# A decoder layer on one core: the down projection as seven block products with weight sums made in DRAM

## The chip, the core and the metric

The kernel runs on one core of a Trainium2 chip. The metric is the device time of one execution in microseconds (us); lower is better. Engine names are those of the profile: PE is the matrix engine, PEld its weight loads, DVE the vector engine, ACT the scalar engine, POOL the general-purpose engine, SP the engine whose queue issues most transfers.

## The reference

One decoder layer on 512 tokens of width 1024 in float32: attention with two branches of 8 heads each (a forgetting softmax branch, "fox", and a stick-breaking branch, "sb"), gates, an output projection, a layer norm, then a gated MLP with a causal convolution of width 3, and a second layer norm. The part that changes is the end:

```python
h_gate, h_val = jnp.split(h, 2, axis=-1)
ffn_out = (jax.nn.silu(h_gate) * h_val) @ w_down
x = _layer_norm(DEEPNORM_ALPHA * x + (1.0 + gt2) * ffn_out, ln2_g, ln2_b)
```

`w_down` is 2816 x 1024, so the product has 512 rows (tokens), an inner dimension of 2816 = 22 x 128 and 1024 columns.

## The kernel before, in words

Every large product is done in three matmuls: each float32 operand is split into a rounded high part (`hi_of`, L74, on ACT) and the rest (`lo_of`, L77, on DVE), and high x high, high x low and low x high are summed in PSUM.

**Weights.** `weights` (L128) is one stream of items of 512 KB for the whole kernel. SP loads them in order into 4 buffers `raw` (L132), ACT makes `wh` (L152) and DVE `wl` (L78 by way of L153) in 3 buffers each. A `raw` buffer is free again when its item has been split; a `wh` buffer when PE has used it. Items are loaded up to 3 ahead of use and split up to 2 ahead.

**Order.** The program is built by a framework that schedules each engine's instructions ahead of time by a model of their costs; SP alone keeps the order of the source. On the chip each engine works through its own list in order, and an instruction that waits holds up all that stand behind it on that engine.

**Stages.** (1) modulation and the first projections; (2) sixteen heads, eight sb then eight fox, in the loop over `heads` (L774), filled up with the remaining projections; each fox head needs two small transfers by POOL (`decay_rows`, L342 and L343); (3) merging of the branches: `merge` (L704) adds on POOL (L706), then splits into `mh` and `ml`; the output weights are scaled on POOL by the gate (`wo_proc`, L601) and split into `woh`, `wol`; (4) output projection and layer norm; (5) the up projection, 44 items of 24 matmuls, each followed by the convolution, and for each pair of items `silu(gate) * value`, split into `hh` and `hl` (L957 to L960); POOL applies the layer norm's row parameters to the residual `x1` in `o_x1` (L887); (6) the down projection: 22 items of `w_down`, each scaled on POOL by the gate (`wdn_proc`, L613), split, and multiplied into 8 PSUM banks (4 blocks of 128 tokens x 2 halves of 512 columns; `down`, L973 to L977). The first 16 items go through all 8 banks; the last 6 (`LATE`) are held split and taken block by block, so that each block's layer norm (L1004 to L1015) runs beside the matmuls of the next. The last half block is cut into two pieces of 256 columns.

SBUF holds 60 buffers `z` of 128 x 512 float32 that all stages share.

Of the kernel before, what the change touches and what calls it, by code (L numbers as in the profile page):

```python
# [16 lines left out]
P = 128  # L17
# [5 lines left out]
FT = DFF // P  # L23
NH = 8
# [13 lines left out]
LATE = 6  # L38
EARLY = 2
# [6 lines left out]
def layer_kernel(ctx: ExitStack, tc: tile.TileContext, out, xT, x, cT, crow, wa0, wa1, bcol, bgt, w1, wct, wv, bf,  # L46
                 wp, wo, lncol, lnrow, wup, cwb, wdn):
# [4 lines left out]
    cons = ctx.enter_context(tc.tile_pool(name="cons", bufs=1))  # L52
    stg = ctx.enter_context(tc.tile_pool(name="stg", bufs=1))
# [74 lines left out]
    def weights(i, ahead=AHEAD):  # L128
        while state["load"] < min(len(items), i + LOADS):
            it = items[state["load"]]  # L130
            it[3] = stg.tile([P, 1024], F32, name=nm("raw"), tag="raw", bufs=LOADS)
            nc.sync.dma_start(it[3][:, 0 : it[2]], it[0])  # L132
            state["load"] += 1
            while state["proc"] <= state["load"] - LOADS:
                process()
# [475 lines left out]
    def wdn_proc(late):  # L611
        def f(r):
            G.tensor_tensor(r, r, gt[1], ALU.mult)  # L613
            if not late:
                h, l = split_proc(r)
                return [h[:, 0:512], h[:, 512:1024]], [l[:, 0:512], l[:, 512:1024]]
            h = [z(F32R, "wdh") for _ in range(2)]
            l = [z(F32R, "wdl") for _ in range(2)]
            for e in range(2):
                c = slice(e * 512, (e + 1) * 512)  # L620
                hi_of(h[e], r[:, c])
                lo_of(l[e], r[:, c], h[e])
            return h, l
# [147 lines left out]
    fill(48)  # L771
    heads = [(br, 2 * p + e) for br, p in seq for e in range(2)]
    last = hd[heads[1]]['last']
    for n, (b, h) in enumerate(heads):  # L774
# [9 lines left out]
        fill(f1)  # L784
        if n + 1 < 16:
# [5 lines left out]
        stage_c(b, h)  # L791
        if n == 7:
# [35 lines left out]
    def ln_row(n):  # L828
# [3 lines left out]
        if n % 2 == 0:  # L832
            for e in range(2):
                G.tensor_scalar(t[e], t[e], -0.5, None, ALU.mult)
# [52 lines left out]
    def o_x1(i):  # L887
        if not lnr:
            lnr.extend([ln_row(0), ln_row(1)])
        for e in range(2):  # L890
            G.tensor_tensor(x1[i][e], x1[i][e], lnr[0][e], ALU.mult)
            G.tensor_tensor(x1[i][e], x1[i][e], lnr[1][e], ALU.add)


    hh, hl = [], []
# [7 lines left out]
    wdi = [add_item(wdn[j], wdn_proc(j >= FT - LATE)) for j in range(FT)]  # L903
# [24 lines left out]

    hc = []
    for n in range(2 * FT):  # L930
# [4 lines left out]
        else:  # L935
# [3 lines left out]
            if n % 2 == 0 and 6 <= n < 14:  # L939
                o_x1((n - 6) // 2)  # L940
            if n in (20, 36):
                g = 6 if n == 20 else 7
                list(ada_split(g, wai[4 * g + 3]))
            if n in (22, 38):
# [5 lines left out]
        hc.append(t)  # L950
        if n % 2 == 1:
# [4 lines left out]
            a, b = z(F32R, "hh"), z(F32R, "hl")  # L956
            hi_of(a, g)  # L957
            lo_of(b, g, a)
            hh.append(a)
            hl.append(b)  # L960
# [4 lines left out]
    lnr = []  # L965
    for i in range(2):
        t = fin.tile([P, D], F32, name=f"ln2_{i}", tag=f"ln2_{i}")
        nc.sync.dma_start(t, lnrow[2 + i : 3 + i, :].broadcast_to([P, D]))
        lnr.append(t)
    G.tensor_scalar(lnr[0], lnr[0], -0.5, None, ALU.mult)  # L970
    acc = [[bank() for _ in range(2)] for _ in range(NB)]

    def down(ps, j, i, w, first, last):  # L973
        tb = slice(i * P, (i + 1) * P)
        PE.matmul(ps, hh[j][:, tb], w[0], start=first, stop=False)  # L975
        PE.matmul(ps, hh[j][:, tb], w[1], start=False, stop=False)  # L976
        PE.matmul(ps, hl[j][:, tb], w[0], start=False, stop=last)  # L977

    own = (NB - 1, 1)
    for j in range(FT - LATE):  # L980
        w = weights(wdi[j])
        for i in range(NB):
            for e in range(2):
                down(acc[i][e], j, i, (w[0][e], w[1][e]), j == 0, (i, e) == own and j == FT - LATE - 1)
    ws = [weights(wdi[j]) for j in range(FT - LATE, FT)]
    for i in range(NB):
        tb = slice(i * P, (i + 1) * P)
        r = x1[i]
# [96 lines left out]
```

## Time and profile before

| what | us |
|---|---|
| median of 3 runs | 765.2 (765.07 to 765.88) |
| span of the profiled execution, first to last instruction | 761.9 |
| what the median has around that span | 3.3 |
| down projection, first to last matmul | 633.9 to 754.1 |
| after the last matmul | 7.8 |

The profiled execution has no time of its own on record beside its span; the median of the runs stands for it. The rows below give busy times per engine, idle time by what ended it, and the time from issue to landing of transfers. A row "a us, b" is total and mean in ns; "x n" is a count; "idle before <-" names what was waited for.

### The profile page before, as it was taken

The page shows a single profiled execution, that of the slowest core. Times are in us where ns is not written, and L with a number is a line of the kernel's source. Part 1 is how long each engine was busy: PE and PEld are TensorE (multiplying, and loading weights), DVE is VectorE, ACT ScalarE, POOL GpSimd, SP SyncE. Part 2 cuts the span into 40 slices and gives each one's busy share as a digit, 9 for nine tenths or more (in the row PEclk, how much of TensorE's full clock was granted, in tenths as well). Part 3 has the DMA queues.
Part 4 walks back from the last instruction along what each step waited for, and adds up shares of the span by engine and source line. Part 5 has one row for each costly group of instructions (what it writes and reads, how often), then busy time and mean ns, then how long its engine had stood idle before and what let it go on. Part 6 is the DMA issues. An engine that isn't in the chain of part 4 may idle for free.

```text
span 761.9 us, 9520 instructions
## 1 busy us (share of the span) xinstructions
PE 747.8 (98%) x3538; PEld 621.3 (82%) x3538; DVE 547.6 (72%) x812; ACT 350.7 (46%) x583; POOL 188.3 (25%) x162
## 2 busy tenths in 40 slices
PE   8999999998999999999999999999999999999995
PEld 4878888877888888888899888888888888888885
DVE  6869799887788985675667697777665765434566
ACT  4567566784866654524145334443444433122300
POOL 1035223542010021362000860000000034845500
PEclk9999999999999999999999999999999999999998
DMA  8944445243332333445203434353323214323202
GB/s 331 405 164 143 162 178 210 83 139 117 106 112 75 120 111 111 138 144 187 90 1 121 156 112 137 111 193 111 139 84 110 84 55 166 139 83 98 97 29 82
DMA packets 31105, 99.68 MB, mean 131 GB/s; under 512 B 4273, under 2 KB 4785, under 8 KB 31058
## 3 DMA queue, kind: packets, MB, share of 16 engines
q1 hardware_dynamic: 30258, 98.72, 36.8%
q8 instruction: 28, 0.46, 0.2%
q10 hardware_dynamic: 288, 0.28, 0.1%
q0 software_dynamic: 512, 0.07, 0.1%
q14 instruction: 19, 0.16, 0.1%
HBM read 96.88 MB, written 2.10 MB: 130 GB/s over the span
## 4 chain that ended last, share of the span: by engine, by line
PE 92%; DVE 4%; DMA 2%; issue 1%; ACT 1%; DVEq 0%; ACTq 0%
PE ps L116 18%; PE ps L118 18%; PE ps L117 18%; PE ps L976 5%; PE ps L975 5%; PE ps L977 5%; PE ps L270 5%; PE ps L521 2%; PE ps L503 2%; PE ps L854 2%; PE ps L855 2%; PE ps L856 2%; DMA raw<-in_wa 1%; PE ps L444 1%; PE ps L445 1%; PE ps L420 1%
## 5 line engine op out<-in xcount | busy, mean ns | idle before, releaser
L78 DVE TENSOR_TENSOR wl<-raw,wh 128x1024 fp32r<-128x1024 f32 (+2 forms) x110 | 150.7, 1371 | 94.5 <-ACT wh L152 94.1
L152 ACT ACTIVATE wh<-raw 128x1024 fp32r<-128x1024 f32 x101 | 106.6, 1057 | 96.8 <-PE ps L977 38.5
L116 PE MATMUL ps<-u2h,wh 128*128 128x512 f32 (+1 forms) x376 | 141.6, 376 | 0.0
L117 PE MATMUL ps<-u2l,wh 128*128 128x512 f32 (+1 forms) x376 | 141.4, 376 | 0.0
L118 PE MATMUL ps<-u2h,wl 128*128 128x512 f32 (+1 forms) x376 | 141.4, 376 | 0.0
L613 POOL TENSOR_TENSOR raw<-raw,gt 128x1024 f32<-128x1024 f32 x22 | 60.1, 2744 | 190.6 <-DVE gt L576 157.7
L117 PEld LDWEIGHTS ps<-u2l,wh 128*128 128x128 f32 x376 | 70.9, 188 | 12.8
L118 PEld LDWEIGHTS ps<-u2h,wl 128*128 128x128 f32 x376 | 70.9, 188 | 12.8
L116 PEld LDWEIGHTS ps<-u2h,wh 128*128 128x128 f32 x376 | 70.9, 188 | 12.6
L116 PE MATMUL ps<-uh,wh 128*128 128x512 f32 x200 | 79.6, 398 | 0.0
L117 PE MATMUL ps<-ul,wh 128*128 128x512 f32 x200 | 78.3, 391 | 0.0
L118 PE MATMUL ps<-uh,wl 128*128 128x512 f32 x200 | 78.2, 391 | 0.0
L976 PE MATMUL ps<-wl,hh 128*128 128x512 f32 x128 | 49.9, 390 | 0.0
L977 PE MATMUL ps<-wh,hl 128*128 128x512 f32 x128 | 49.9, 390 | 0.0
L975 PE MATMUL ps<-wh,hh 128*128 128x512 f32 x128 | 49.9, 390 | 0.0
L483 POOL TENSOR_TENSOR pt<-pt,om 128x127 f32<-128x127 f32 (+3 forms) x32 | 42.7, 1346 | 10.8 <-DVE om L482 9.7
L118 PEld LDWEIGHTS ps<-uh,wl 128*128 128x128 f32 x200 | 37.6, 188 | 8.2
L116 PEld LDWEIGHTS ps<-uh,wh 128*128 128x128 f32 x200 | 37.7, 188 | 7.3
L117 PEld LDWEIGHTS ps<-ul,wh 128*128 128x128 f32 x200 | 37.7, 189 | 7.1
L75 ACT ACTIVATE hh<-cv 128x512 fp32r<-128x512 f32 x22 | 13.9, 631 | 59.6 <-DVE cv L955 59.6
L954 ACT ACTIVATE cv<-cv 128x512 f32<-128x512 f32 x22 | 13.9, 632 | 56.5 <-DVE cv L949 56.5
L601 POOL TENSOR_TENSOR raw<-raw,gt 128x1024 f32<-128x1024 f32 x8 | 20.7, 2596 | 77.1 <-DMA raw<-in_wo 75.9
(185 smaller groups left out, 1511.6 us busy)
## 6 DMA issues: line engine op xcount, KB each, us to landing
raw<-in_wup SPq DMA_DIRECT2D x44, 512.0 KB, 3.2
raw<-in_wa SPq DMA_DIRECT2D x32, 512.0 KB, 3.3
raw<-in_wct SPq DMA_DIRECT2D x25, 512.0 KB, 3.2
raw<-in_wdn SPq DMA_DIRECT2D x22, 512.0 KB, 3.3
wa<-in_wa SPq DMA_DIRECT2D x14, 512.0 KB, 7.9
raw<-in_wv SPq DMA_DIRECT2D x8, 512.0 KB, 3.4
raw<-in_wp SPq DMA_DIRECT2D x8, 512.0 KB, 3.3
raw<-in_wo SPq DMA_DIRECT2D x8, 512.0 KB, 3.2
```

Of the source, the lines that this page charges most:

```text
L78: return V.tensor_tensor(o, i, fl(hi), ALU.subtract)
L116: PE.matmul(ps, wh, ah, start=first, stop=False)
L117: PE.matmul(ps, wh, al, start=False, stop=False)
L118: PE.matmul(ps, wl, ah, start=False, stop=last)
L152: state["hi"] = S.activation(h[:, 0:cols], r[:, 0:cols], AF.Copy)
L270: PE.matmul(grp[g], w, u, start=j == 0 and n == 0, stop=j == KT - 1 and n == (1 if g == 7 else 2))
L483: G.tensor_tensor(pt[b][:, s : e - 1], pt[b][:, s : e - 1], om[:, s + 1 : e], ALU.mult)
L601: G.tensor_tensor(r, r, gt[0], ALU.mult)
L613: G.tensor_tensor(r, r, gt[1], ALU.mult)
L975: PE.matmul(ps, hh[j][:, tb], w[0], start=first, stop=False)
L976: PE.matmul(ps, hh[j][:, tb], w[1], start=False, stop=False)
L977: PE.matmul(ps, hl[j][:, tb], w[0], start=False, stop=last)
```

## The change

The down projection is cut into 2 x 2 x 2 blocks: 2 halves of the tokens (256), the inner blocks taken in 11 pairs (even, odd), 2 halves of the columns (512). A scheme of Strassen's kind then needs 7 block products instead of 8. The sums of activations that it needs are made per pair on POOL in `blocks`, four subtractions or additions of 128 x 256, and then split; the sums of weights are made in DRAM: ACT copies weights to scratch tensors (`down_copy`, one pair per head, in the loop over the heads) and POOL issues transfers that add to what stands there (`down_sum`, written in the up projection's loop). Each of the three transfers of a pair reads what the one before it wrote, and waits for it.

Three operands of each of the first 8 pairs (`oh`, `ol`, `sp`) are stored to DRAM (`keep`) and fetched back into `z` buffers by POOL's queue (`back`); the residual `x1` also goes to DRAM and back. The gate is no longer applied to the weights, but for 6 late items, scaled on POOL and stored in the up stage (`scale_proc`); otherwise it is applied to the results, by POOL in `fold` and by DVE in `gated`. The products come in four parts: A (`ai`, 11 items of 12 matmuls), B (`bi`, 11 of 12), D (`dci`, 5 of 12 and 1 of 6), C (`ci`, 5 of 12), then the last 6 pairs of C row block by row block from `cli`.

In the built program the framework has put all 33 adding transfers of `down_sum` into POOL's list between the fox heads and the first `merge`, not into the up projection.

```diff
+    def down_copy(n, e):
+        if 0 <= n - 5 < FP:
+            with tc.issue_after(state["hi"].ins):
+                S.dma_start((w31, w24)[e][n - 5], wdp[n - 5][:, e * 1024 : (e + 1) * 1024])
+    def down_sum(n):
+        if n < FP:
+            G.dma_start(w31[n], wdp[n][:, 2048:3072], accum_op=ALU.add)
+        if 0 <= n - 1 < FP:
+            G.dma_start(wt2[n - 1], w31[n - 1][:, 0:512], accum_op=ALU.add)
+        if 0 <= n - 2 < FP:
+            G.dma_start(wt4[n - 2], wt2[n - 2], accum_op=ALU.add)
...
-            hi_of(a, g)
-            lo_of(b, g, a)
+            if n % 4 == 3:
+                work = blocks(*hs)
+    def blocks(e, o):
...
+        hi_of(oh, o)
+        lo_of(ol, o, oh)
+        G.tensor_tensor(g[:, lo], e[:, hi], e[:, lo], ALU.subtract)
+        G.tensor_tensor(g[:, hi], o[:, lo], e[:, lo], ALU.subtract)
+        G.tensor_tensor(e[:, lo], g[:, hi], e[:, hi], ALU.add)
+        G.tensor_tensor(s4[:, lo], o[:, hi], e[:, lo], ALU.subtract)
...
+        hi_of(gh, g)
+        lo_of(gl, g, gh)
...
+        hi_of(eh, e)
+        lo_of(el, e, eh)
+        hi_of(sp[:, lo], s4[:, lo])
+        lo_of(sp[:, hi], s4[:, lo], sp[:, lo])
...
+    def fold(i, e, t, sign):
+        G.tensor_tensor(t, t, (g0, g1)[e], ALU.mult)
+        G.tensor_tensor(r[i][e], r[i][e], t, sign)
...
+    for i in range(2):
+        V.tensor_tensor(u3[i], u2[i], Z[i], ALU.add)
+    for i in range(2):
+        V.tensor_tensor(c22[i], u3[i], W[i], ALU.add)
+        V.tensor_tensor(u2[i], u2[i], W[i], ALU.add)
...
+    for i in range(2):
+        fold(i, 0, u3[i], ALU.add)
+        fold(i, 1, c22[i], ALU.subtract)
...
+    def gated(i, e, ps):
+        t = fine("t")
+        V.tensor_tensor(t, ps, (g0, g1)[e], ALU.mult)
+        V.tensor_tensor(r[i][e], r[i][e], t, ALU.add)
...
+    for p in range(FP - LATE):
+        oh, ol, sp = keeps[p]
+        w = weights(ci[p])
...
+        if p % 2 == 0 and p < 4:
+            fold(2 + p // 2, 1, u2[p // 2], ALU.subtract)
+            first_rows(p // 2)
+    for q in range(LATE):
+        wc[q] = weights(cli[q])
+    for i in range(2):
+        gated(2 + i, 0, X[i])
+        gated(2 + i, 1, W[i])
```

More of the change, by code (lines that the diff above doesn't have):

```diff
@@ L23 @@
 FT = DFF // P
+FP = FT // 2
+H = T // 2
 NH = 8
@@ L38 @@
 LATE = 6
+STAY = 3
 EARLY = 2
@@ L950, in layer_kernel @@
         hc.append(t)
+        if n > 3:
+            next(work, None)
         if n % 2 == 1:
```

252 lines of the change are left out of this document (183 added, 69 removed).

## The prediction

> **What bounds the kernel now.** First the page: its span, the busy time per engine, and the chain of work that ended last, by engine.
>
> ```profile
> span 761.9 us, 9520 instructions
> PE 747.8 (98%) x3538; PEld 621.3 (82%) x3538; DVE 547.6 (72%) x812; ACT 350.7 (46%) x583; POOL 188.3 (25%) x162
> ...
> PE 92%; DVE 4%; DMA 2%; issue 1%; ACT 1%; DVEq 0%; ACTq 0%
> ```
>
> PE carries 92% of the chain. An average over stages can hide another limit in one of them, so next the table by stage for the stretches that the change touches: the heads with the branches' merge, two of the up projection, the down projection, the end.
>
> ```profile
> core 0: us, PE busy (x) PEld busy (x) DVE busy (x) ACT busy (x) POOL busy (x), PEclk, DMA share, GB/s
> 172.00:310.00 138.00, 135.60 (x701) 113.38 (x700) 108.12 (x201) 84.60 (x172) 17.27 (x18) 1.00 0.33 108
> ...
> 405.00:450.00 45.00, 45.00 (x220) 38.12 (x219) 38.10 (x38) 20.29 (x27) 28.93 (x18) 1.00 0.40 141
> 450.00:500.00 50.00, 50.00 (x222) 41.45 (x221) 36.71 (x46) 22.46 (x30) 0.00 (x0) 1.00 0.37 127
> ...
> 633.90:754.10 120.20, 120.16 (x547) 99.97 (x545) 63.92 (x75) 25.10 (x33) 54.86 (x20) 1.00 0.30 106
> ...
> 754.00:762.00 8.00, 0.06 (x1) 0.00 (x0) 4.49 (x13) 0.29 (x1) 0.00 (x0) 0.66 0.19 66
> ```
>
> In the down projection PE is busy for 120.16 of 120.20 us at full granted clock (1.00), while DVE works 63.92 us, half of it. So a matmul less is time less there, but only until DVE has become the busier one. That is the question of this change.
>
> **Step 1, the matmuls: 15.0 us less on PE.** Durations of single matmuls overlap, so their spacing counts. Two rows of PE's timeline, the first and the last of 97 matmuls in a row, and the counts of one of the three product lines:
>
> ```profile
> 609.65 0.39 PE L117 MATMUL ps<-u2l,wh 128*128 128x512 f32 x1
> ...
> 631.41 0.39 PE L117 MATMUL ps<-u2l,wh 128*128 128x512 f32 x1
> ```
> ```profile
> L975 PE MATMUL ps<-wh,hh x128: 388/390/390, 633.9 to 720.3; 128*128 128x512 f32 x128
> ...
> L975 PE MATMUL ps<-wdh,hh x54: 278/389/390, 721.0 to 753.5; 128*128 128x512 f32 x42, 128*128 128x256 f32 x12
> ```
>
> (631.41 - 609.65) / 96 = 0.2267 us. Before: 3 x (128 + 42) = 510 full matmuls and 3 x 12 = 36 half ones; the halves come out at (120.2 - 115.6) / 36 = 0.13 us. After: 7 products x 11 pairs x 2 blocks x 3 = 462, of which 18 are again cut into 36 halves: 444 x 0.2267 + 4.6 = 105.3 us. 66 matmuls go, 66 x 0.2267 = 15.0 us. If PE stays the bound, this is the gain. In times from the stage's start: A ends at 29.9, B at 59.9, D (66 matmuls) at 74.8, C (60) at 88.4, the last rows at 105.3.
>
> **Step 2, DVE from the end of B: it becomes the bound, and takes back 12.1 us.** Rows of DVE and POOL in the stages before, whose operations are those of the new stage:
>
> ```profile
> 457.47 0.69 DVE L955 TENSOR_TENSOR cv<-cv,cv 128x512 f32<-128x512 f32 x1
> ...
> 702.68 1.21 DVE L78 TENSOR_TENSOR wl<-raw,wh 128x1024 fp32r<-128x1024 f32 x1
> 703.82 1.28 DVE L78 TENSOR_TENSOR wdl<-raw,wdh 128x512 fp32r<-128x512 f32 x2
> ...
> 725.31 0.69 DVE L1004 SCALAR_TENSOR_TENSOR xn<-xn,ps 128x512 f32<-128x512 f32 x1 [2.39 <-PE ps L977]
> 726.03 0.69 DVE L1005 BATCH_NORM_STATS2 st<-xn 128x6 f32<-128x512 f32 x1
> ...
> 730.84 0.21 DVE L819 BATCH_NORM_AGGREGATE mv<-st 128x2 f32<-128x12 f32 x1
> ...
> 734.45 0.68 DVE L1004 SCALAR_TENSOR_TENSOR xn<-xn,ps 128x512 f32<-128x512 f32 x1
> ```
> ```profile
> 441.44 1.77 DVE L955 TENSOR_TENSOR cv<-cv,cv 128x512 f32<-128x512 f32 x1
> 443.13 2.32 DVE L78 TENSOR_TENSOR wl<-raw,wh 128x1024 fp32r<-128x1024 f32 x1
> ```
> ```profile
> 302.75 1.30 POOL L706 TENSOR_TENSOR sg<-sg,sg 128x512 f32<-128x512 f32 x1
> ...
> 439.13 3.53 POOL L891 TENSOR_TENSOR xn<-xn,lnr 128x512 f32<-128x512 f32 x2
> 442.62 3.98 POOL L892 TENSOR_TENSOR xn<-xn,lnr 128x512 f32<-128x512 f32 x2
> ```
>
> By the distance to the next start, a full split costs 703.82 - 702.68 = 1.14 us, a half one 0.64, an operation with a PSUM operand or a row statistic 0.72, and a row's norm from its aggregate to its last write 734.45 - 730.84 = 3.6. In the built order DVE, once B's last product is there, has: u3, the split of D's second item and u3 again, which end at 59.9 + 1.3 = 61.2; then four operations on PSUM (2.9); eight full splits and one half (9.1 + 0.6); twelve half splits of the late items (7.7); six `gated` pairs (6 x (0.72 + 0.64) = 8.2); statistics and norms of two rows (4 x 0.72 + 7.2 = 10.1); and, before the last addition, row 2 and the start of row 3: nine operations of 512 columns at 0.72 (6.5) and about 2.3 of small ones (8.8). Sum 47.4, which puts the last addition at 108.6 us with DVE never idle, against 105.3 for PE.
>
> POOL runs beside it: twelve `fold` operations (1.30 us alone), four of them while DVE reads PSUM, eight beside its splits. The four rows at 439 to 443 us show what that does when both read SBUF: 1.77 for 0.69 and 2.32 for 1.23, 1.1 us more each. Eight such delays are 8.7 us (bounds: 0, and 8 x 1.30 = 10.4). The last addition then starts at 61.2 + 47.4 + 8.7 = 117.3 us, where before it started right after PE's last matmul at 120.2. Behind it stands the same end, 7.8 us. **So 2.9 of the 15.0 us are left.** PE will wait in C above all, for the splits of C's items, which stand in DVE's list behind the late items' splits and the two row norms.
>
> **Step 3, the adding transfers on POOL's queue: taken at 0, but with no cover.** The trace of before has no such transfer. Nearest rows, from the list of transfers:
>
> ```profile
> raw<-in_wdn SPq DMA_DIRECT2D x22, 512.0 KB, 3.3
> wa<-in_wa SPq DMA_DIRECT2D x14, 512.0 KB, 7.9
> ...
> xn<-in_x SPq DMA_DIRECT2D x8, 256.0 KB, 2.8
> ...
> s<-chi POOLq DMA_DIRECT2D x8, 4.0 KB, 1.6
> ```
>
> Each pair has one of 512 KB (A us) and two of 256 KB (B us); the second waits on POOL for the first, the third for the second. In the built list they stand ahead of the last fox heads' small transfers, of the output weights' scaling (L601) and of the first merge (L706). Nearest in time are these:
>
> ```profile
> 258.55 0.59 ACT L527 ACTIVATE ytmp<-ps 64x512 f32<-64x512 f32 x1
> ...
> 270.73 0.59 ACT L527 ACTIVATE ytmp<-ps 64x512 f32<-64x512 f32 x1 [2.47 <-PE ps L521]
> ...
> 304.08 0.63 ACT L75 ACTIVATE mh<-sg 128x512 fp32r<-128x512 f32 x1 [4.52 <-POOL sg L706]
> ...
> 307.36 1.06 ACT L152 ACTIVATE wh<-raw 128x1024 fp32r<-128x1024 f32 x1 [0.17 <-PE ps L117]
> ...
> 323.68 1.06 ACT L152 ACTIVATE wh<-raw 128x1024 fp32r<-128x1024 f32 x1 [0.61 <-PE ps L117]
> ```
>
> A head takes 270.73 - 258.55 = 12.2 us, and one pair is copied per head, so POOL keeps up while A + B, with 1 us of issuing, stays under 12.2. The copies of pairs 8 to 10 are issued near 269 to 291. Pair 8 can be added from some 274 on; with the second scaling (2.6), the first merge then ends at about 282 + 3A + 2B. Before it ended at 304.05, and ACT's `mh` waited for it. How late may it be? The two `wh` rows bracket three items on PE (307.2 to 323.1, 5.3 each); the second of these is needed at 312.5, and after the merge ACT and DVE need 3.9 us for it (`mh`, two `woh`, `wh`, `wl`). So a stall is 3A + 2B - 26.6, if positive. Bounds: A from 3.3 (a plain load) to 15.8 (twice the crowded load of 7.9); B from 2.8 to 7.9. I take A = 6.0 and B = 4.3: two loads' time less one latency of 1.6 for the 512 KB (5.0) and for the 256 KB (4.0), and 1 and 0.3 for traffic beside it. That is 26.6, a stall of 0, at the very edge. The heads' small transfers have slack: POOL issued a head's rows at 181, and its scores came at 237.6, 56 us later.
>
> ```profile
> 181.32 0.52 POOL L342 DMA_DIRECT2D s<-chi  x1 [5.20 <-PE ps L450]
> ```
> ```profile
> 237.62 0.24 PE ps L445
> ```
>
> On what an addition costs there is a rule in the Trainium skill, Collectives: The Full Stack, section "The bandwidth ceiling: the fold count and why AG ≠ RS ≠ AR": a reducing transfer has to read two sources, and so runs at half a copy's rate. By it alone A would be 5.0 and B 4.0 and the stall none, the sum the same; no trace of before shows such a transfer.
>
> **Step 4, the rest, taken at 0.** Up projection: per four items (21.8 us) DVE has 36.71 / 50 x 21.8 = 16.0 us, to which come one half split and one of 256 columns (1.05), and up to 2.6 of waiting for four POOL operations (half of 1.30 each): 19.7 of 21.8. At 405 to 450 us DVE was 85% busy beside a busy POOL and PE lost nothing, so that cover holds, narrowly. Parts A and B: an item per 2.72 us needs 1.14 on DVE and 1.06 on ACT, and a load of 3.3 with four buffers. What is fetched back (9 MB in 60 us) doubles the traffic to some 350 GB/s; were one load as late as the 7.9 us row, that is 4.6 us, once. So 0 to 5.
>
> **Sum.** 761.9 of span - 15.0 + 12.1 = 759.0; with the 3.3 us around the span, which I take from the median, **762.3 us** against 765.2, 0.4% faster.
>
> **The rivals.**
> - *Slower: the adding transfers hold POOL.* Above 3A + 2B = 26.6 (A + B about 10.3) the first merge is late, and ACT and then PE behind it; above A + B = 13 the earlier pairs lag too. At A = 9 and B = 6 the last pairs cost 39 - 26.6 = 12.4. The first copy lands near 172 us by its place in ACT's list; eight pairs of 14 us (A + B less the 1 us by which the next pair starts ahead) end at 284, 10 later than the 274 above. Together 22: 762.3 + 22 = 784. At A = 10, B = 7 the same sum gives 43, 805. For: the DMA share is already 0.33 there, 22 copies of 512 KB come on top, and each addition passes through memory more often than a load. Against: at the price of loads, 11 x (3.3 + 2 x 2.8) = 98 us of transfers fit into the 130.
> - *Faster: PE stays the bound.* If DVE and POOL get past each other and DVE's list has less in it than I count, the full 15.0 comes: 750 to 757. Against it: 47.4 us of DVE work in 45.4 of PE's even without a single delay.
> - *No change: DVE is fully shut out.* If each of the eight splits waits for a whole POOL operation, 10.4 goes instead of 8.7: 764.0; with a stall or two of Step 4 up to 767. The Trainium skill, SBUF — State Buffer, section "Who interferes with whom", makes this the rule: the pair of ports that the two engines share is locked for a whole instruction. The rows at 439 to 443 us, with 1.1 for 1.30, come near it.
>
> **How the numbers follow.** About 0.2% (1.5 us) is what a measurement of this kernel can tell from no change. Chances: forecast (758 to 763.6) 0.35; POOL held 0.41; PE the bound 0.11; no change 0.13. So faster 0.35 + 0.11 = 0.46, same 0.13, slower 0.41. At the far bounds (A 15.8, B 7.9) the first rival's sum is over 100 us; I leave 0.15 of it above 788, and 0.05 of the second below 752. Range: 752 to 788. The forecast's own range is 758 to 763.6.
>
> **What would show it.** Step 1: 444 + 36 matmuls in the last stage at the same spacing. Step 2: PE idle in C, ended by `wl`; `wl` at 2.3 us beside `fold`. Step 3: A and B as the time from issue to landing; POOL idle for transfers between 230 and 310 us, and `mh` waiting for POOL. Step 4: no PE idle in the up projection, A and B. Wrong it would be if A + B is over 11, or if C shows no wait of PE.

## The result, and the profile after

The changed kernel takes 791.3 us (median of 4 runs, 788.1 to 795.1) against 765.45 for the kernel before in the same series: a ratio of 1.0344, 95% interval 1.0312 to 1.0376. It is 3.4% slower. The forecast was 762.3 us, 0.4% faster, with a range up to 788; the rival "the adding transfers hold POOL" was priced at 784. The profiled execution is the run of 788.1 us, with a span of 786.4. Line numbers below are those of the changed kernel; a kernel with a few lines more or less shows the same statements one to six lines further up or down.

First the page of the changed kernel: span, busy time per engine, and the engines' shares of the chain that ended last.

```profile
span 786.4 us, 9844 instructions
PE 746.1 (95%) x3472; PEld 614.0 (78%) x3472; DVE 588.9 (75%) x866; ACT 375.4 (48%) x624; POOL 271.3 (35%) x285
...
PE 67%; DVE 12%; DMA 10%; issue 5%; POOL 2%; ACT 2%; SPq 0%; DVEq 0%; POOLq 0%; ACTq 0%
```

PE has 66 instructions fewer and is the chain for 67% of the span, where it was 92%. Transfers now carry 10%. So the time is not in the new products but in waits elsewhere. The table by stretches shows where; first two of the kernel before, cut at the same events, then the changed kernel.

```profile
222.50:296.00 73.50, 73.50 (x394) 62.09 (x393) 58.73 (x113) 43.87 (x93) 6.54 (x4) 1.00 0.29 99
296.00:345.20 49.20, 49.16 (x217) 40.32 (x217) 33.28 (x36) 20.41 (x32) 22.47 (x11) 1.00 0.40 135
```
```profile
core 0: us, PE busy (x) PEld busy (x) DVE busy (x) ACT busy (x) POOL busy (x), PEclk, DMA share, GB/s
...
229.00:304.50 75.50, 74.87 (x393) 61.86 (x393) 61.13 (x116) 43.05 (x92) 15.98 (x18) 1.00 0.92 257
304.50:371.00 66.50, 55.43 (x218) 43.93 (x217) 35.33 (x35) 18.32 (x30) 30.15 (x19) 0.87 0.58 152
...
664.60:694.60 30.00, 30.00 (x134) 24.85 (x133) 20.84 (x21) 15.58 (x19) 20.22 (x30) 1.00 1.03 358
694.60:725.40 30.80, 30.10 (x133) 24.61 (x132) 18.75 (x14) 11.68 (x11) 10.13 (x14) 1.00 0.97 334
725.40:761.00 35.60, 31.34 (x130) 25.10 (x129) 34.42 (x45) 16.90 (x23) 22.35 (x14) 0.95 0.56 183
```

The same 217 or 218 matmuls of the merge stretch take 66.5 us instead of 49.2. In the heads before it the DMA share has gone from 0.29 to 0.92. The down projection's parts A and B run with one wait of PE, 0.70 us in B; in part C (from 725.4) DVE is busy for 34.42 of 35.60 us.

What holds the merge is on POOL. The adding transfers stand in its list from 176.75 us on, among the small transfers of the fox heads. Its timeline, columns start, length, and in brackets the idle time before and what ended it; L797, L799 and L801 are the three adding transfers of a pair, L614 the scaling of the output weights, L724 the merge:

```profile
275.51 0.81 POOL L797 DMA_DIRECT2D w<-in_wdp  x1 [0.84 <-DMA w<-in_wdp]
...
290.16 1.15 POOL L797 DMA_DIRECT2D w<-in_wdp  x1
300.13 0.81 POOL L799 DMA_DIRECT2D w<-w  x1 [8.82 <-DMA w<-in_wdp]
307.08 0.81 POOL L801 DMA_DIRECT2D w<-w  x1 [6.14 <-DMA w<-w]
307.62 2.64 POOL L614 TENSOR_TENSOR raw<-raw,gt 128x1024 f32<-128x1024 f32 x1
...
329.21 0.81 POOL L801 DMA_DIRECT2D w<-w  x1 [3.19 <-DMA w<-w]
329.76 1.55 POOL L724 TENSOR_TENSOR sg<-sg,sg 128x512 f32<-128x512 f32 x1
```

The second scaling starts at 307.62 (282.4 before) and the first merge at 329.76 (302.75 before), each directly behind an adding transfer that waited for the one ahead of it. The list of the tile that the transfers write gives POOL's idle time before all 33 of them, by what ended it (us, times):

```profile
  DMA w<-in_wdp: 66.5, 15
  DMA w<-w: 46.4, 11
```

That is 113 us of waiting between 176 and 329 us. The first kind covers two things, a pair's own first addition and the copies that ACT issues: seven of the fifteen waits, 25 us, ended when a copy landed. The last of these seven is the row at 275.51 above. Behind the merge wait ACT and then PE, in the timelines of these two:

```profile
331.34 0.63 ACT L84 ACTIVATE mh<-sg 128x512 fp32r<-128x512 f32 x1 [23.04 <-POOL sg L724]
```
```profile
334.00 0.79 PE L125 MATMUL ps<-yh,wh 128*128 128x512 f32 x1 [6.15 <-ACT wh L165]
...
337.15 0.63 PE L125 MATMUL ps<-yh,wh 128*128 128x512 f32 x1
337.58 0.63 PE L126 MATMUL ps<-yl,wh 128*128 128x512 f32 x1
```

`wh`, which PE needs, stands behind `mh` in ACT's list. After the wait PE's matmuls come at a spacing of 337.58 - 337.15 = 0.43 us instead of 0.23. The loss of the stretch has these two parts: PE is idle for 66.50 - 55.43 = 11.1 us, and its matmuls are 55.43 - 49.16 = 6.3 us longer. Of the idle time 6.15 and 1.33 us stand behind the merge. Another 3.27 stand, at 312 us, behind the low part `yl` on DVE, which waited 1.51 us for a load of modulation weights and then worked on it for 3.26 us (1.22 in the median) beside POOL's late scaling.

The span's 24.5 us by stretches, cut at first and last matmuls of tiles: `yh` first (the second projections of the sb branch, 222.6 before and 229.0 after), last `ptc` (end of the heads), first `woh` (output projection), first `u2h` (up projection), first `eh` or `hh` (down projection), last matmul, end. The same table for all runs is used in the next section (us of each one profiled execution; where two kernels do the same, their profiles agree to 2.1 us in the first column and to 0.3 in the heads, merge and output columns):

| kernel | to `yh` | heads | merge | output | up | down | tail | span |
|---|---|---|---|---|---|---|---|---|
| before | 222.6 | 73.4 | 49.5 | 46.1 | 242.3 | 119.9 | 8.1 | 761.9 |
| changed | 229.0 | 75.4 | 66.8 | 47.9 | 245.7 | 112.4 | 9.2 | 786.4 |
| e1_late | 227.9 | 73.4 | 49.8 | 46.0 | 255.4 | 115.3 | 9.1 | 776.9 |
| e2_plain | 230.4 | 73.4 | 53.7 | 50.6 | 247.3 | 111.4 | 9.2 | 776.0 |
| e3_dve | 228.7 | 76.6 | 54.3 | 46.1 | 247.4 | 111.7 | 9.2 | 774.0 |
| e4_nosum | 225.8 | 73.4 | 49.8 | 46.1 | 245.8 | 111.9 | 9.2 | 762.0 |
| e5_nocopy | 222.7 | 73.3 | 49.5 | 46.1 | 247.4 | 111.6 | 9.1 | 759.7 |
| e6_nofold | 223.9 | 73.5 | 49.5 | 46.1 | 247.3 | 106.7 | 9.1 | 756.1 |
| e7_x1 | 223.5 | 73.4 | 49.5 | 46.1 | 242.3 | 111.7 | 9.1 | 755.6 |
| e8_spread | 223.7 | 73.4 | 49.1 | 46.1 | 251.5 | 114.7 | 9.2 | 767.7 |
| e9_thin | 222.5 | 73.4 | 49.1 | 46.1 | 251.8 | 118.5 | 9.2 | 770.6 |
| e10_early | 224.0 | 75.5 | 49.1 | 46.1 | 251.4 | 116.8 | 9.2 | 772.1 |
| e11_nochain | 230.4 | 74.4 | 57.2 | 46.1 | 247.3 | 113.7 | 9.2 | 778.3 |
| e12_ring | 228.0 | 74.6 | 49.2 | 46.1 | 248.9 | 120.0 | 8.7 | 775.5 |
| e13_ring_after | 230.9 | 83.1 | 68.5 | 49.7 | 248.7 | 111.4 | 9.2 | 801.5 |
| e14_ring_bare | 228.1 | 73.4 | 49.5 | 46.1 | 242.4 | 113.2 | 9.6 | 762.3 |
| e15_tiny | 224.1 | 73.4 | 49.1 | 46.1 | 242.3 | 111.7 | 9.2 | 755.9 |
| e16_plain_late | 223.7 | 73.4 | 49.1 | 46.1 | 244.9 | 117.1 | 8.7 | 763.0 |

For the change: 6.4 + 2.0 + 17.3 + 1.8 + 3.4 - 7.5 + 1.1 = 24.5 us.

### The profile page after: what moved, and what is told of

The parts are those of the page before. It is cut to its first block, busy times and chain, and to the rows that moved or that the text cites. A ratio compares the mean times of both kernels' runs of the same rounds, so it can differ in the third digit from the quotient of the medians.

```text
span 786.4 us, 9844 instructions
## 1 busy us (share of the span) xinstructions
PE 746.1 (95%) x3472; PEld 614.0 (78%) x3472; DVE 588.9 (75%) x866; ACT 375.4 (48%) x624; POOL 271.3 (35%) x285
## 3 DMA queue, kind: packets, MB, share of 16 engines
q0 software_dynamic: 10832, 25.24, 13.7%
## 4 chain that ended last, share of the span: by engine, by line
PE 67%; DVE 12%; DMA 10%; issue 5%; POOL 2%; ACT 2%; SPq 0%; DVEq 0%; POOLq 0%; ACTq 0%
PE ps L127 15%; PE ps L125 15%; PE ps L126 15%; PE ps L283 4%; DMA raw<-in_wa 4%; DMA w<-in_wdp 3%; DVE wl L87 3%; PE ps L1078 2%; PE ps L1079 2%; PE ps L1077 2%; PE ps L891 1%; PE ps L516 1%; PE ps L892 1%; DMA w<-w 1%; PE ps L890 1%
## 5 line engine op out<-in xcount | busy, mean ns | idle before, releaser
L87 DVE TENSOR_TENSOR wl<-raw,wh 128x1024 fp32r<-128x1024 f32 (+2 forms) x127 | 173.8, 1372 | 64.5 <-ACT wh L165 62.5
L165 ACT ACTIVATE wh<-raw 128x1024 fp32r<-128x1024 f32 (+1 forms) x118 | 124.3, 1053 | 95.3 <-PE ps L1079 31.8
L125 PE MATMUL ps<-uh,wh 128*128 128x512 f32 x200 | 81.5, 408 | 0.1
L127 PE MATMUL ps<-uh,wl 128*128 128x512 f32 x200 | 80.2, 401 | 0.0
L993 POOL TENSOR_TENSOR sg<-cv 128x256 f32<-128x256 f32 x11 | 11.9, 1080 | 96.7 <-DVE cv L1049 96.6
L183 DVE SCALAR_TENSOR_TENSOR raw<-raw,cbc 128x1024 f32<-128x1024 f32 x16 | 23.7, 1479 | 21.5 <-DMA raw<-in_wa 21.5
L1039 ACT ACTIVATE cv<-ps,cw 128x512 f32<-128x512 f32 x44 | 33.5, 761 | 2.5 <-PE ps L127 2.5
L125 PE MATMUL ps<-yh,wh 128*128 128x512 f32 x64 | 26.8, 419 | 6.9 <-ACT wh L165 6.2
L1041 DVE SCALAR_TENSOR_TENSOR cv<-ps,cw,cv 128x510 f32<-128x510 f32 x44 | 32.8, 744 | 0.8
L87 DVE TENSOR_TENSOR ml<-sg,mh 128x512 fp32r<-128x512 f32 x8 | 8.8, 1096 | 32.6 <-ACT mh L84 32.6
```

The lines of the kernel that those rows point to most:

```text
L87: return V.tensor_tensor(o, i, fl(hi), ALU.subtract)
L125: PE.matmul(ps, wh, ah, start=first, stop=False)
L127: PE.matmul(ps, wl, ah, start=False, stop=last)
L165: state["hi"] = S.activation(h[:, 0:cols], r[:, 0:cols], AF.Copy)
L183: return V.scalar_tensor_tensor(wt[:, c], wt[:, c], 1.0, cbc[:, c], ALU.mult, ALU.mult, accum_out=o)
L1039: S.activation(t, ps, AF.Identity, bias=cw[:, n, 3:4], scale=cw[:, n, 2:3])
```

## The experiments

Theory H: the adding transfers hold POOL's in-order queue. Theory C: copies and additions crowd the weight loads. Each time is the median, with the ratio to the kernel before in the same series and its 95% interval.

**Where the additions stand, and what they cost as a whole.** Four runs on the changed kernel. In e1_late `state["g"]` is the first POOL operation of `blocks` (L993):

```diff
-                down_sum((n - 12) // 2)
+                with tc.issue_after(state["g"].ins):
+                    down_sum((n - 12) // 2)
```

> The 33 adding transfers are tied behind the feed-forward blocks' first POOL operation, so that they stand in the up projection as the program text has them, each set of three spread over three pairs; nothing else moves. Theory H (the adding transfers hold POOL's in-order queue, and the scaling and the merge behind it come late): the 17.3 us that the stretch from the last head to the output projection lost come back, the first merge starts within 5 us of 303 us, and the whole is 766 to 775 us. Theory C (the copies and additions crowd the weight loads, wherever they stand): the loss moves into the up projection, whose 245 us grow by 10 or more, and the whole stays above 783 us.

Measured 779.05 us, 1.018 (1.0163 to 1.0197). This is between the two ranges. The merge stretch is back at 49.8 us, as H says, but the up projection has grown by 9.7 to 255.4, as C says. Each theory holds for a part.

e2_plain, on all three lines of `down_sum`:

```diff
-            G.dma_start(w31[n], wdp[n][:, 2048:3072], accum_op=ALU.add)
+            G.dma_start(w31[n], wdp[n][:, 2048:3072])
```

> The 33 adding transfers become plain copies at the same places with the same waits (it leaves out the addition of the weights). If an addition's second read is what makes A = 7.8 and B = 5.7 us, they fall to about 5 and 4, A + B = 9 is under the 10.3 at which the merge is late, and the whole is 768 to 776 us. If their time is that of the crowded queues and of the wait for landing, A stays above 6.5 and B above 5, the first merge stays 20 us late, and the whole is 783 to 792 us.

Measured 778.04 us, 1.0175 (1.0148 to 1.0201). The median times from issue to landing, of the changed kernel and of this one, and the software queue's row (packets, MB, share of the 16 engines' span) of the changed kernel, of this one and of e4_nosum:

```profile
w<-in_wdp POOLq DMA_DIRECT2D x11, 512.0 KB, 7.8
w<-w POOLq DMA_DIRECT2D x22, 256.0 KB, 5.7
...
q0 software_dynamic: 10832, 25.24, 13.7%
```
```profile
q0 software_dynamic: 9424, 25.24, 9.8%
...
w<-in_wdp POOLq DMA_DIRECT2D x11, 512.0 KB, 5.2
w<-w POOLq DMA_DIRECT2D x22, 256.0 KB, 4.3
```
```profile
q0 software_dynamic: 6080, 13.70, 5.2%
```

The time to landing falls to 5.2 and 4.3, which is the branch of the second read, and the merge stretch gives back 13.1 of its 17.3 us. The total is 2 us above the branch's range; the first column (230.4) and the output column (50.6) have not come back. By engine time, the 25.24 - 13.70 = 11.5 MB of sums took 0.137 x 786.4 - 0.052 x 762.0 = 68.1 us of the sixteen engines as additions and 0.098 x 776.0 - 39.6 = 36.4 us as copies: 1.87 times as much per byte.

e3_dve, in `merge` and `wo_proc`:

```diff
-            G.tensor_tensor(m, m, ma[j], ALU.add)
+            V.tensor_tensor(m, m, ma[j], ALU.add)
...
-        G.tensor_tensor(r, r, gt[0], ALU.mult)
+        V.tensor_tensor(r, r, gt[0], ALU.mult)
```

> The scaling of the output weights and the merges of the two branches move from POOL to DVE; the adding transfers stay where they are with all their traffic. Theory H: POOL's queue then holds nothing that PE waits for but the heads' small transfers, 12 to 17 us come back, 772 to 780 us. Theory C: the traffic is the same, so is the loss, 785 to 793 us.

Measured 774.7 us, 1.0118 (1.0089 to 1.0148). 12.5 us of the merge stretch come back with all the additions in place, on an engine that had to take up 16 operations more. H is confirmed for that part; the rest of the loss stays, in the columns before and in 54.3 against 49.5.

e4_nosum:

```diff
-            if 12 <= n < 16 + 2 * FP and n % 2 == 0:
-                down_sum((n - 12) // 2)
```

> No adding transfers at all (it leaves out the sums of the weights: parts A, B and D multiply by the copied blocks); the 22 copies stay. Theory H: the heads' stage is as before but for the copies, and the time is 758 to 766 us. Theory C splits by which traffic crowds: if the copies do it, the stretch up to the first gate projection of the second branch still comes 5 us or more late, and the time is over 764 us; if only the additions do, it is 758.

Measured 766.54 us, 1.0024 (1.0005 to 1.0042), 0.5 us above H's range. All additions together cost 791.3 - 766.5 = 24.8 us. The copies alone still bring the first column to 225.8 (227.9 in e1_late, where they are also alone before it), and the up projection keeps 3.5 us of loss that has nothing to do with either.

**The parts that remain without sums.** Three runs on a base without copies and sums, in which the items of A, B and (likewise) D read blocks of the input. e5_nocopy:

```diff
-    ai.append(add_item([wdc[p][:, 0:512], wt2[p]], split_proc))
+    ai.append(add_item([wdc[p][:, 0:512], wdp[p][:, 1024:1536]], split_proc))
...
-    bi.append(add_item(w31[p], split_proc))
+    bi.append(add_item(wdp[p][:, 0:1024], split_proc))
```

> Neither copies nor adding transfers (it leaves out the sums of the weights; parts A, B and D read unsummed blocks of the input at the same sizes). The stretch up to the second branch's first gate projection then starts its yh matmuls at 222.6 us as before, if the copies' traffic cost the 3.2 us of the run without sums; at 225 or more if something else in the rebuilt order did. The down projection with its tail stays 7 us shorter than before, the up projection 3.5 us longer: span 757 to 760, time 759 to 763 us.

Measured 762.7 us, 0.9969 (0.9956 to 0.9982). The first column is 222.7: the copies' traffic was its loss, 3.1 us in the spans and 3.8 in the medians.

e6_nofold, on that base, in `fold`:

```diff
-        G.tensor_tensor(t, t, (g0, g1)[e], ALU.mult)
-        G.tensor_tensor(r[i][e], r[i][e], t, sign)
+        pass
```

> As the run without copies and sums, and POOL's twelve scaling and adding operations of the last stage left out (so the final rows lack those products). The forecast's Step 2: DVE bounds the end and POOL beside it costs it 8.7 us, so the last addition comes 5 to 9 us earlier than in the run with them, until PE's 105.3 us is the bound. Rival: DVE's own list bounds it alone and POOL runs in gaps; then the stage shrinks by less than 2 us.

Measured 758.09 us, 0.9906 (0.9891 to 0.992). The down projection falls from 111.6 to 106.7 us, 4.9 us, just below the expected 5 to 9, close to PE's 105.3. The splits beside `fold` are the reason, by DVE's and POOL's timelines in the changed kernel:

```profile
734.57 3.40 DVE L87 TENSOR_TENSOR wl<-raw,wh 128x1024 fp32r<-128x1024 f32 x2
737.90 3.48 DVE L87 TENSOR_TENSOR wdl<-raw,wdh 128x512 fp32r<-128x512 f32 x2
741.30 2.28 DVE L87 TENSOR_TENSOR wl<-raw,wh 128x1024 fp32r<-128x1024 f32 x1
743.50 3.46 DVE L87 TENSOR_TENSOR wdl<-raw,wdh 128x512 fp32r<-128x512 f32 x2
```
```profile
737.39 1.75 POOL L1102 TENSOR_TENSOR r<-r,u 128x512 f32<-128x512 f32 x1
739.09 1.74 POOL L1102 TENSOR_TENSOR r<-r,c 128x512 f32<-128x512 f32 x1
740.79 3.94 POOL L1101 TENSOR_TENSOR u<-u,gt 128x512 f32<-128x512 f32 x2
```

and in e6_nofold, where nothing of POOL runs:

```profile
703.60 2.36 DVE L87 TENSOR_TENSOR wl<-raw,wh 128x1024 fp32r<-128x1024 f32 x2
...
711.23 1.29 DVE L87 TENSOR_TENSOR wdl<-raw,wdh 128x512 fp32r<-128x512 f32 x2 [0.80 <-ACT wdh L84]
```

Two half splits take 1.29 us alone and 3.46 beside POOL.

e7_x1, on that base; `state["g"]` is the last POOL operation of `blocks`:

```diff
-                o_x1((n - 6) // 4, n // 2 % 2 == 0)
+                with tc.issue_after(state["g"].ins):
+                    o_x1((n - 6) // 4, n // 2 % 2 == 0)
```

> As the run without copies and sums, with the layer norm's second half on POOL tied behind the blocks' operations of the same stretch, so that these 20 operations no longer stand ahead of the second group's blocks. If they are why ACT waited 12.3 us for POOL and PE 2.8 us at the slower clock behind it, the up projection falls from 245.8 to 242.5 us and the whole by 3 us; if the wait only moves to a later group, it stays within 1 us.

Measured 757.84 us, 0.9921 (0.99 to 0.9942). The up projection falls from 247.4 to 242.3 us, the value of the kernel before. POOL's, ACT's and PE's timelines without the fix (e4_nosum) show the chain:

```profile
458.35 1.29 POOL L927 TENSOR_TENSOR xn<-xn,lnr 128x512 f32<-128x512 f32 x1
459.60 0.74 POOL L993 TENSOR_TENSOR sg<-cv 128x256 f32<-128x256 f32 x1
460.29 0.73 POOL L994 TENSOR_TENSOR sg<-cv,cv 128x256 f32<-128x256 f32 x1
```
```profile
461.06 0.63 ACT L84 ACTIVATE gh<-sg 128x512 fp32r<-128x512 f32 x1 [12.26 <-POOL sg L994]
```
```profile
464.80 0.50 PE L125 MATMUL ps<-u2h,wh 128*128 128x512 f32 x1 [2.32 <-ACT wh L165]
```

The scheduler had put the residual's 20 operations ahead of the second group's `blocks`; ACT waited 12.26 us for them in `gh`, with the next `wh` behind it.

**The whole computation again, without the hold.** e8_spread has the fix of e7_x1 and in addition

```diff
-        if 0 <= n - 5 < FP:
+        for p in range(max(n - 8, 0) * FP // 8, max(n - 7, 0) * FP // 8):
...
-            if 12 <= n < 16 + 2 * FP and n % 2 == 0:
-                down_sum((n - 12) // 2)
+            if n >= 4 and (n - 4) % 3 == 0:
+                with tc.issue_after(state["g"].ins):
+                    down_sum((n - 4) // 3)
```

(with `p` for `n - 5` in `down_copy`).

> The whole computation: copies from the ninth head on, adding transfers in the up projection at every third item from the fifth, behind the blocks' operations, and the layer norm's second half spread as in the run beside it. Theory: the hold of POOL's queue is gone as in the first run that moved the sums (17 us), the first copies no longer meet the crowded loads near 182 us (2 to 3 us), and a thinner traffic in the up projection costs less than the 9.6 us it cost there: 764 to 772 us. Rival: the up projection has no room for this traffic however it is spread, 10 us or more stay, 773 to 779 us.

Measured 771.46 us, 1.0083 (1.0064 to 1.0103). All columns up to the output projection are those of the kernel before; the copies, begun at 207 instead of 168 us, cost nothing any more. The up projection stays 9.2 us above e7_x1. Two rows of e7_x1 and of this kernel place it:

```profile
500.00:520.00 20.00, 20.00 (x89) 16.53 (x89) 13.91 (x17) 8.10 (x12) 6.77 (x5) 1.00 0.72 231
520.00:540.00 20.00, 20.00 (x89) 16.52 (x88) 16.93 (x23) 10.21 (x16) 4.17 (x4) 1.00 0.58 184
```
```profile
500.00:520.00 20.00, 16.16 (x69) 12.42 (x67) 11.48 (x13) 6.76 (x10) 8.19 (x9) 0.96 1.05 260
520.00:540.00 20.00, 18.25 (x73) 14.90 (x74) 16.87 (x21) 8.25 (x13) 9.57 (x9) 0.87 0.81 219
```

The DMA engines are full in the first of these stretches (a share of 1.05), and DVE waits for a load of modulation weights with PE's `wl` behind it: 6.98 us, where e7_x1 shows 3.29.

```profile
519.02 1.54 DVE L568 SCALAR_TENSOR_TENSOR ac<-raw,cTs,ac 128x512 f32<-128x512 f32 x2 [6.98 <-DMA raw<-in_wa]
```
```profile
505.90 1.54 DVE L568 SCALAR_TENSOR_TENSOR ac<-raw,cTs,ac 128x512 f32<-128x512 f32 x2 [3.29 <-DMA raw<-in_wa]
```

PE's timeline of e8_spread shows the wait behind it:

```profile
521.75 0.80 PE L127 MATMUL ps<-u2h,wl 128*128 128x512 f32 x1 [5.37 <-DVE wl L87]
```

In all of its up projection PE is idle for 6.4 us, in this wait and two more for `wl` (0.78 and 0.22); e7_x1 has none. Behind the long wait eight matmuls come at a spacing of 0.41 to 0.59 us. Together with them that one wait makes up 7.5 of the 9.2 us in this execution.

e9_thin, the second argument choosing one of the three transfers:

```diff
-            if n >= 4 and (n - 4) % 3 == 0:
+            if 4 <= n < 43:
                 with tc.issue_after(state["g"].ins):
-                    down_sum((n - 4) // 3)
+                    down_sum((n - 4) // 3, (n - 4) % 3)
```

> The whole computation, as the run with spread transfers, but the three adding transfers of a step stand at three successive items of the up projection instead of all at one, so at most 512 KB are asked for at once. The spread run lost its 9.2 us of the up projection between 500 and 545 us, where loads of modulation weights took up to 11 us beside such bursts. If bursts are the cause, the up projection falls from 251.5 to about 245 us, 764 to 767 us in all; if the sum of the traffic is, it stays at 250 or more, 769 to 773 us.

Measured 772.65 us, 1.0101 (1.0084 to 1.0119). The up projection is at 251.8: not the bursts. No adding transfer waits on POOL in this run, so the loss is no hold of its queue either. The down projection is longer as well (118.5); PE's longest wait in its part A, 3.03 us, stands behind ACT, which waited 5.22 us for operations of `blocks` on POOL.

e10_early, on e9_thin:

```diff
         fill(f1)
+        if 11 <= n < 14:
+            for m in range(3):
+                down_sum(n - 11, m)
...
-            if 4 <= n < 43:
+            if 4 <= n < 43 - 9:
                 with tc.issue_after(state["g"].ins):
-                    down_sum((n - 4) // 3, (n - 4) % 3)
+                    down_sum((n - 4) // 3 + 3, (n - 4) % 3)
```

> As the run beside it, and the additions of the first pairs moved ahead into the last heads, before the first scaling of the output weights, where POOL's queue has nothing that PE waits for soon and the copies' traffic alone runs; the up projection has that much less. If the hold only hurts once it reaches the scaling and the merge, this costs the heads 0 to 2 us and gives the up projection 1 to 3 us: 761 to 766 us. If any addition beside the heads' loads costs PE, the heads lose 3 us or more and nothing is won, 765 to 772 us.

Measured 770.16 us, 1.0064 (1.0043 to 1.0086), the lowest median of a whole version, though within the scatter of e8_spread. The heads lose 2.1 us, between the two branches, and the up projection wins nothing. No whole version here beats the kernel before.

e11_nochain, on the changed kernel, lets the second and third transfer of a pair add blocks of the input:

```diff
-            G.dma_start(wt2[n - 1], w31[n - 1][:, 0:512], accum_op=ALU.add)
+            G.dma_start(wt2[n - 1], wdp[n - 1][:, 2048:2560], accum_op=ALU.add)
...
-            G.dma_start(wt4[n - 2], wt2[n - 2], accum_op=ALU.add)
+            G.dma_start(wt4[n - 2], wdp[n - 2][:, 2560:3072], accum_op=ALU.add)
```

> The changed kernel with its additions at the same places, of the same sizes and with the same traffic, but the second and third of a pair read blocks of the input instead of the result of the one before (so other sums are formed than the scheme's), and wait only for the copies. Theory H (the waits of one adding transfer for another hold the queue): the first merge comes 12 to 20 us earlier and the whole is 772 to 779 us. Theory C (traffic): nothing of the traffic is gone, 786 to 793 us.

Measured 777.91 us, 1.0173 (1.0154 to 1.0191): within H's range. With the same bytes the merge stretch gives back 9.6 us. The first merge starts at 316.33, 13.4 us earlier, and POOL no longer holds it: it waited 6.89 us for `sg` from DVE. The 7.7 us of loss that stay in the stretch are of another kind. PE's longest wait there is for `yl` (the only other one, for `yh`, is 1.41 us). DVE made `yl` late because it waited for a load of modulation weights:

```profile
314.30 0.79 PE L126 MATMUL ps<-yl,wh 128*128 128x512 f32 x1 [4.13 <-DVE yl L87]
```
```profile
312.40 1.23 DVE L183 SCALAR_TENSOR_TENSOR raw<-raw,cbc 128x1024 f32<-128x1024 f32 x1 [4.38 <-DMA raw<-in_wa]
```

**What the traffic acts through.** e12_ring, on e8_spread, in `weights` (`state["ada"]` lists the sources of the modulation weights' items, `NZ` is the number of `z` buffers); e13_ring_after is the same edit on the changed kernel and e14_ring_bare on e7_x1:

```diff
-NZ = 60
+NZ = 58
...
-            it[3] = stg.tile([P, 1024], F32, name=nm("raw"), tag="raw", bufs=LOADS)
+            ada = any(it[0] is w for w in state.get("ada", []))
+            it[3] = stg.tile([P, 1024], F32, name=nm("raw"), tag="ada" if ada else "raw", bufs=1 if ada else LOADS)
```

> The run with spread transfers, and the modulation weights' loads get a buffer of their own, so that they are asked for one item earlier and the ring of four is left to the projections' weights; for the room the pool of small tiles has 58 instead of 60. If the 9 us of the up projection are the uncovered time to landing of these loads (DVE waited 19.8 us for four of them, against 4.7 without the additions), DVE's waits fall under 8 us and the up projection to 242 to 246 us, 761 to 766 us in all. If the DMA engines are simply full, the waits move to the projections' loads and the up projection stays at 249 or more, 768 to 773 us.

Measured 773.53 us, 1.0111 (1.0068 to 1.0155). Up projection 248.9: only 2.6 of the 9.2 us. DVE still waits 16.1 us for these loads, so the buffer did not do what it was to do.

> The changed kernel with nothing but that buffer (and 58 small tiles). Theory of the uncovered loads: the stretch to the second branch's first gate projection falls from 229 to 225 us or less and the heads from 75.4 to 73.4; the hold of POOL stays, so 783 to 787 us. Theory of full DMA engines: 788 to 793 us.

Measured 802.46 us, 1.0488 (1.0458 to 1.0519). Against both theories: the heads grew by 7.7 us, with DVE waiting up to 8.4 us for the very loads that had got the buffer. Whether one buffer is too few for them in that traffic was not tried, so this run decides nothing.

> The control: that buffer in the run without copies and sums and with the spread layer norm, 757.8 us there (it leaves out the sums of the weights). Nothing waits long for these loads there (4.7 us in the up projection, with no wait of PE), so both theories expect 756 to 759 us; if it is over 760, the two tiles fewer cost something themselves and are to be taken off the other two runs.

Measured 763.96 us, 0.9989 (0.9974 to 1.0005). The control is 6 us above its counterpart e7_x1, 4.6 of them before `yh`. So the edit has a cost of its own, and of e12_ring only the up column is read, where the control shows none (242.4).

e15_tiny, on e8_spread, on all three lines of `down_sum`:

```diff
-            G.dma_start(w31[n], wdp[n][:, 2048:3072], accum_op=ALU.add)
+            G.dma_start(w31[n][0:16], wdp[n][0:16, 2048:3072], accum_op=ALU.add)
```

> The run with spread transfers, its 33 adding transfers at the same places with the same waits, but of 16 rows each instead of 128 (it leaves out most of the sums). If the traffic costs the 9 us, the up projection falls to 242 to 244 us and the whole to 759 to 762 us; if POOL's issuing of additions does, beside DVE or ahead of the blocks, the up projection stays at 249 to 252 us, 768 to 772 us.

Measured 758.23 us, 0.992 (0.99 to 0.994), up projection 242.3; the total is just below the branch's range and 0.4 us above e7_x1. The same 33 instructions at the same places with an eighth of the bytes cost nothing: it is the traffic, not POOL's issuing of it.

e16_plain_late, on e8_spread, makes the edit of e2_plain:

```diff
-            G.dma_start(w31[n], wdp[n][:, 2048:3072], accum_op=ALU.add)
+            G.dma_start(w31[n], wdp[n][:, 2048:3072])
```

> The same run with whole transfers, plain copies instead of additions (it leaves out the sums). In the heads the software queue's transfers took 13.7% of the sixteen engines' time with the additions and 9.8% without, about half per byte of a sum. If the second read carries the cost, the up projection falls by 4 us or more, to 247 or less, 763 to 767 us; if any transfer of this size there costs as much, it stays at 249 to 252 us.

Measured 761.15 us, 0.9954 (0.9936 to 0.9971), faster than the range, up projection 244.9. So 6.6 of the 9.2 us of this column come with the second read of the additions, and 2.6 with the bytes of a plain copy. By medians of the whole it is 10.3 (e8_spread to here) and 2.9 us (here to e15_tiny). The down projection does not follow: 114.7 in e8_spread, 117.1 here, 111.7 in e15_tiny. What lengthens it was not separated.

## Why the prediction was wrong, step by step

**Step 1, 66 matmuls and 15.0 us: right.** PE's list has the 480 new products; part A took 694.7 - 664.8 = 29.9 us, as forecast. With `fold` left out the stage took 106.7 us of the forecast 105.3.

**Step 2, DVE as the bound from the end of B: right in place and cause, somewhat too dear.** PE's long waits, 2.64 and 1.61 us, are in C and for `wl`, in the changed kernel:

```profile
743.63 0.50 PE L1078 MATMUL ps<-wl,bk 128*128 128x512 f32 x1 [2.64 <-DVE wl L87]
```

The delay beside `fold` was put at 8.7 us. The nine splits from 728.5 to 746.9 us (the second of the row at 734.57 is a half one) lost 1.97 + 1.55 + 2.12 + 1.06 + 2.11 = 8.8 against the prediction's prices, and DVE was idle once, 1.18 us for a result of `fold`. The last addition started 113.9 us into the stage, forecast 117.3: the sum of DVE's own list was some 4 us too high. Most of that is the price of 0.72 for an operation of 512 columns; back to back they came every 0.60 us here. The gain of the stage with its tail is 6.4 us (7.5 less 1.1), forecast 2.9. The tail was taken as unchanged; it is 1.1 longer.

**Step 3, the adding transfers at 0: this step failed, and made the sign wrong.** The mechanism was named, and given 0.41 as a rival. What failed first is the price of a transfer: A = 6.0 and B = 4.3 were taken from loads; measured were 7.8 and 5.7 in the changed kernel, and 5.2 and 4.3 as plain copies (e2_plain). The forecast's own sentence "at the very edge" should have moved its chance: at A + B = 13.5 the point of 10.3 is passed. The Trainium skill's rule quoted there, in Collectives: The Full Stack, section "The bandwidth ceiling: the fold count and why AG ≠ RS ≠ AR", that an addition reads two sources and so goes at half a copy's rate, is stated there for collectives; the 1.87 times the engine time per byte found here agrees with it. The times of 5.0 and 4.0 that the prediction drew from it were too low all the same. The loads that they were made of ran beside a DMA share of 0.30 (the down projection before), the additions beside 0.92. They also went from DRAM into SBUF and not from DRAM to DRAM; how much is due to which was not separated.

The second term that failed is the start. The prediction adds pair 8 from 274 us on; its first addition was issued at 290.16, 16 us later. Its copy landed only at 284.39, in heads that themselves ran 8.4 us late (229.0 + 75.4 against 222.6 + 73.4). The other 5.8 us are the queue's: up to pair 7 POOL still waited for copies, so it kept up, and only from pair 8 on was it behind. From there the formula is close: with the measured A and B, 290.2 + 8 + 3A + 2B gives 333.0 for the end of the first merge, measured 331.3. At 3A + 2B - 26.6 alone the stall would be 8.2 us; the merge started 27.0 late, 8.4 of it with the heads, and the stretch lost 17.3. The hold is not all of that: without the chain 9.6 us came back (e11_nochain), with the merge and the scaling on DVE 12.5 (e3_dve), and the long wait that stayed in e11_nochain was for a late load, which is the next point.

**What no step had: the loads that the additions slow.** For the heads the prediction treated traffic as a delay of the additions themselves. It is dear in the other direction too: 9.2 us in the up projection, where PE waits for nothing that POOL's queue holds (e8_spread against e7_x1, and e15_tiny against e8_spread; in e9_thin no addition waits there at all). So no place was found in this kernel where the sums are free: of their 24.8 us, moving them brought back about half, and e8_spread is still 13.6 us above e7_x1, which has none.

**Step 4, the rest at 0 with a bound of 5: wrong by two terms.** The copies cost 3.1 us in the spans where they begin too early (e5_nocopy against e4_nosum; the column scatters by 2.1) and 3.8 in the medians, and the residual's operations ahead of `blocks` hold ACT, 3.5 to 5.1 us (e7_x1). The cover that was checked, DVE's 19.7 of 21.8 us, was not what gave way; ACT's list behind POOL was, and no row of ACT was read there. Parts A and B and their loads at 350 GB/s cost nothing but the 0.70 us in B, as forecast.

**The sum's 3.3 us around the span** are not all around it: in every run with its own span on record that part is 1.7 to 2.1 us. The rest is the distance of the profiled execution before from the median of the runs; since the forecast starts from the median, this changes nothing in it.

Taken out one after the other, the additions (24.8 us), the copies (3.8) and the residual's place (4.9) lead, in medians, from 791.3 to 757.8 us, which is 7.3 below the median of the kernel before. That is what the seven products would be worth here if their sums were free. The three were removed in this order only; in another order the single prices could differ.

What stays open: how to cover the loads that the additions slow. In the profiled execution of e8_spread one late load of modulation weights is behind 7.5 of the 9.2 us. An own buffer for these loads (e12_ring) left most of DVE's waits for them in place, and its control was disturbed by the smaller pool.

## What to carry to other kernels

Price an added transfer twice: by how long the queue that issues it stands behind its landing, and by what its bytes do to every load that runs beside it; a summing transfer counts for nearly two copies. Where a framework hoists such instructions into an in-order list, look at what stands behind them there, not at where the source has them. A forecast that finds its key number "at the very edge" of a threshold has no ground to call the cost nothing.

## What the runs showed of the hardware that was not expected

An addition from DRAM to DRAM takes 1.87 times the DMA engines' time of a copy per byte, and POOL issues one in 0.8 to 0.9 us in the median (changed kernel), a plain copy in 0.5 (e2_plain).

After a wait PE can lose twice. In e5_nocopy a wait of 2.32 us and one of 0.53 were followed by seven matmuls at a spacing of 0.43 us, and the up projection lost 5.1 us instead of 3.5; the same two waits in e4_nosum were not. The rows are those of e5_nocopy:

```profile
461.26 0.50 PE L125 MATMUL ps<-u2h,wh 128*128 128x512 f32 x1 [2.32 <-ACT wh L165]
462.53 0.50 PE L127 MATMUL ps<-u2h,wl 128*128 128x512 f32 x1 [0.53 <-DVE wl L87]
...
463.87 0.63 PE L125 MATMUL ps<-u2h,wh 128*128 128x512 f32 x1
464.29 0.63 PE L126 MATMUL ps<-u2l,wh 128*128 128x512 f32 x1
```

The granted clock in the ten microseconds around it is 0.83. The Trainium skill, TensorE: Matmul & The Clock Gate, section "Part 1: The HAM clock gate (the "warmup" mystery)", has the array fall to half rate after an idle window of about 3.4 us. Here 2.3 and 0.5 us of idle did it once and once not, so a wait shorter than that is not safe by its length alone. A single wait in part C shows the same: after 2.64 us in e7_x1 the spacing was 0.43 us, after 2.65 us in e8_spread it stayed at 0.23. A column of one profile can differ by a microsecond or two for this reason alone.
